# Conformer convolution on one Trainium2 core: 11 of 31 taps moved from TensorE to VectorE, ScalarE and GpSimd, and a wider second projection group

## The chip, the cores and the metric

The kernel runs on one core of one Trainium2 chip. The metric is the device time of one execution in microseconds (us). Before the change the median of three runs is 2734.93 us (2734.37 to 2735.12).

The engines are named as in the profile: PE is TensorE (PEld its weight loads), DVE is VectorE, ACT is ScalarE, POOL is GpSimd, and SP is the engine whose queue issues most transfers.

## What is computed

The reference is one step of a small hybrid decoder: an attention layer with a ConvFFN behind it, then a Conformer convolution layer with a second ConvFFN behind it. A prompt of 256 tokens and eight samples of 4 tokens share all weights, 288 columns in all. The model width is 2048, in 16 tiles of 128 channels. The change touches the Conformer layer alone:

```python
def conformer_conv(x, hist, w_pw1, b_pw1, w_dw, b_dw, ln_g, ln_b, w_pw2, b_pw2):
    a, gate = jnp.split(x @ w_pw1 + b_pw1, 2, axis=-1)
    a = a * jax.nn.sigmoid(gate)
    a_pad = jnp.concatenate([hist, a], axis=1)
    h = jax.nn.silu(layer_norm(causal_dwconv(a_pad, w_dw, b_dw), ln_g, ln_b))
    return h @ w_pw2 + b_pw2, a_pad[:, -(CONV_WIDTH - 1):]
```

`causal_dwconv` is a depthwise convolution over time with 31 taps: each output of a channel is the sum of 31 products of that channel's own values with that channel's own weights, and a bias. The history of the prompt is zero; the samples have a history of 30 rows.

## The kernel before

**Matrix products.** Channels lie on partitions and tokens along the free dimension. The core routine `gemm_gen` walks through a group of weight columns in slabs of 512 KB. For each slab, `pump` issues the transfer into a buffer `raw` (L145, SP's queue), ACT rounds it into a high part `wh` (L159), and DVE subtracts to get the low part `wl` (L161). PE then makes three matmuls per weight tile and depth step: wh by xh (L228), wh by xl (L229) and wl by xh (L230). Five `raw` and three `wh`/`wl` buffers let the split run two slabs ahead of PE, so a `wh` has to wait until PE has left the slab three before it.

**Order of the side work.** Everything else is written as generators in lanes. After each row of matmuls `tick` credits every lane with PE time and lets it issue what its credit covers (the numbers that are yielded are such times). `ev` holds the evacuation of the last group, `norms` the normalization of the layer's input, `bg` the convolutions, and `bg2` the preparation of a convolution, which starts only when `ev` is empty. All engines work in the order of issue.

**The first projection (pw1).** Group 0 holds the columns of tiles 0 and 1 and of their gates, four blocks of 128. Every later group holds one tile and its gate, two blocks. Group 0 is multiplied with the input before its normalization, and `after` (L526, L529) corrects the result. Group 1 is the first that reads the normalized input: `normed` makes it tile by tile (DVE and POOL at L484, POOL at L486, ACT at L470 and L473), ending in the low part `xl` on DVE (L476), and PE needs all 16 tiles in turn.

**The convolution of tiles 0 to 14.** `glu` makes the gated tile `apad` (sigmoid on ACT, L1552; product on DVE, L1553). `spread_out` writes it to a scratch tensor in DRAM (L1583), has POOL build small diagonal weight blocks `dg` (L1586, 1024 elements a partition), adds the samples' four products on DVE (L1573) and reads the scratch back four times with four shifts into `xt` (L1593). In `xt` 32 channels by 4 shifts fill the partitions, so that a block matmul does four taps at once; `conv` needs 8 steps of 4 column blocks, 32 matmuls (L1605). The result is evacuated by ACT for tiles 0 to 3 (L1609) and by DVE for tiles 4 to 14 (L1617 from PSUM with the centre `lnc` taken off, and L1619 for the 32 sample columns). `shifted` then feeds the layer norm's sums (ACT L298, POOL L303 and L304).

**The last tile.** `conv_last` does not go through DRAM. 14 taps (`NDG`) are full diagonal matmuls on PE (L1644), 4 (`NPOOL`) are products on ACT, added in pairs by POOL (L1640) and brought in by PE (L1646), and 13 run on DVE (L1653). Then come a sum (L1657), the last statistics matmuls (L331, L332) and the layer norm in front of pw2.

Of the kernel before, what the change touches and what calls it, by code (L numbers as in the profile page):

```python
# [7 lines left out]
F32 = mybir.dt.float32  # L8
# [4 lines left out]
AF = mybir.ActivationFunctionType  # L13
OP = mybir.AluOpType
AX = mybir.AxisListType

D = 2048
NT = 16
TP = 256
NS, TS = 8, 4  # L20
# [8 lines left out]
CW = 31  # L29
# [7 lines left out]
CH = 22  # L37
NKVB = 3
FILL = 0.45
NPOOL = 4  # L40
CAP = 3.0
SDEL = 6
TOPK = 2.6
KG = 12
DGP = 6.0
NDG = 14
CQ = 287
BIS = (1.6, 0.2)
DOTS = 0.35
ROPE = 0.8  # L50
# [8 lines left out]
CLAG = (3.2, 5.6, 5.0, 1.0)  # L59
# [474 lines left out]
def trunk(ctx, tc, a, o, stages=9):  # L534
    k = K(ctx, tc, a, o)
    nc = k.nc
# [12 lines left out]
    def halving(w, nk):  # L549
        return [k.add(Group([(w, 512 * i, 512)], [128] * 4, nk, 2)) for i in range(3)] + \  # L550
            [k.add(Group([(w, 1536 + 256 * i, 256)], [128] * 2, nk, 4)) for i in range(2)]
# [9 lines left out]
    def ffn_groups(l):  # L561
        wg, wu, wd = a["w_ffn_gate"][l], a["w_ffn_up"][l], a["w_ffn_down"][l]
        r = []
        for c in range(NF // CH):
            ga = [k.add(Group([(wg, (c * CH + 2 * i) * 128, 256), (wu, (c * CH + 2 * i) * 128, 256)],
                              [128] * 4, NT, 2)) for i in range(CH // 2)]
            wdc = wd[c * CH * 128:(c + 1) * CH * 128, :]
            gb = (halving if c and not l else narrowing)(wdc, CH)
            r.append((ga, gb))
        return r  # L570

    g_f0 = ffn_groups(0)
    g_pw1 = [k.add(Group([(a["w_pw1"], 0, 256), (a["w_pw1"], D, 256)], [128] * 4, NT, 2))]
    g_pw1 += [k.add(Group([(a["w_pw1"], 128 * j, 128), (a["w_pw1"], D + 128 * j, 128)], [128] * 2, NT, 4))
              for j in range(2, NT)]
    g_pw2 = halving(a["w_pw2"], NT)
    g_pw2[0].slabs[1].pool = True
    g_f1 = ffn_groups(1)
# [223 lines left out]
    def sample_index():  # L802
# [58 lines left out]
        def total():  # L861
            p_ = pb()
            nc.tensor.matmul(p_[:, :1], cc("bones"), cnt, start=True, stop=True)
            return p_

        nc.vector.tensor_scalar(scr, S, 0.0, 0.0, op0=OP.is_ge, op1=OP.add, accum_out=cnt)
        yield BIS[0]
        p = total()
        yield BIS[1]
        nc.vector.tensor_scalar(v, p[:, :1], float(KSEL_S), -1.0, op0=OP.is_lt, op1=OP.mult)  # L870
        for bit in range(30, -1, -1):
# [96 lines left out]
    acc = [bp.tile([128, 128 * (tt + 1)], F32, name=f"pacc{tt}") for tt in range(2)]  # L968
# [97 lines left out]
    def bank(n, bufs):  # L1066
        return pp.tile([128, 512], F32, name=n, bufs=bufs)
# [3 lines left out]
    for gi in range(2):  # L1071
# [430 lines left out]
    fp = sf.enter_context(tc.tile_pool(name="ffn0", bufs=1))  # L1502
# [15 lines left out]
    fp = sf.enter_context(tc.tile_pool(name="conf", bufs=1))  # L1518
    cy = fp.tile([128, NT, T], F32, name="cy")
    last = NT - 1  # L1520

    lpad = fp.tile([128, 286], F32, name="lpad")
    diag = fp.tile([128, NDG, 128], F32, name="diag")
    nident = fp.tile([128, 128], F32, name="nident")

    spread = tc.dram_tile([last * 128, CQ], F32, name="spread")
    zero = fp.tile([128, last, CW], F32, name="zero")
    tapm = fp.tile([128, 32], F32, name="tapm")
    wdq = fp.tile([128, NT * 32], F32, name="wdq")
    pads = {}  # L1530
# [8 lines left out]
    def glu(js, ps):  # L1539
        n = len(js)  # L1540
        for m, j in enumerate(js):
            if j == last:
                t = lpad[:, 30:]
            else:
                t = pads[j] = fp.tile([128, TP], F32, name="apad", bufs=4)
            sg = fp.tile([128, T], F32, name="sg", bufs=2)
            pa, pg_, ba, bg_ = ps[m], ps[n + m], k.par("b_pw1", j), k.par("b_pw1", 16 + j)
            if type(pa) is tuple:
                for (_, w_), b_ in ((pa, ba), (pg_, bg_)):
                    nc.gpsimd.tensor_tensor(w_, w_, b_, op=OP.add)  # L1550
                (pa, ba), (pg_, bg_) = pa, pg_
            nc.scalar.activation(sg, pg_[:, :T], AF.Sigmoid, bias=bg_)  # L1552
            nc.vector.scalar_tensor_tensor(t, pa[:, :TP], ba, sg[:, :TP], op0=OP.add, op1=OP.mult)  # L1553
            nc.vector.scalar_tensor_tensor(hist[:, j, :, CW - 1:], pa[:, TP:T].rearrange("p (s w) -> p s w", w=4),
                                           ba, sg[:, TP:].rearrange("p (s w) -> p s w", w=4),
                                           op0=OP.add, op1=OP.mult)
            yield 0.7

    def diags():
        nc.scalar.activation(nident, k.ident, AF.Copy, scale=-1.0)  # L1560
        yield DGP
        for q_ in range(NDG):
            nc.scalar.activation(diag[:, q_], k.ident, AF.Copy, scale=k.par("w_dw", last * CW + q_))
# [13 lines left out]

    def spread_out(j):

        t = pads.pop(j)  # L1580
        nc.gpsimd.tensor_copy(tailp[:, j], t[:, TP - CW + 1:])
        rows = spread[j * 128:(j + 1) * 128]
        nc.sync.dma_start(rows[:, CW:], t)  # L1583
        dg = fp.tile([128, 32, 32], F32, name="dg", bufs=2)
        wq = wdq[:, 32 * j:32 * j + 32]
        nc.gpsimd.tensor_tensor(dg, wq[:, :, None].to_broadcast([128, 32, 32]),  # L1586
                                tapm[:, None, :].to_broadcast([128, 32, 32]), op=OP.mult)
        for d in range(TS):
            samples(j, d)
            yield CLAG[0] / TS  # L1590
        xt = fp.tile([128, 4, 284], F32, name="xt", bufs=3)
        for i in range(4):
            nc.sync.dma_start(xt[32 * i:32 * i + 32], rows[:, i:i + 284].rearrange("(g c) u -> c g u", c=32))  # L1593
        yield CLAG[1]
        spreads[j] = dg, xt

    def conv(j):

        while j not in spreads:
            yield 0.3  # L1600
        dg, xt = spreads.pop(j)
        p = pp()
        for m in range(8):
            for i in range(4):
                nc.tensor.matmul(p[32 * i:32 * i + 32, :TP], dg[:, 8 * i + m], xt[:, i, 4 * m:4 * m + TP],  # L1605
                                 start=m == 0, stop=m == 7, skip_group_check=True)
        yield CLAG[2]
        if j < lnc.H:
            nc.scalar.activation(cy[:, j, :TP], p[:, :TP], AF.Identity, bias=k.par("b_dw", j))  # L1609
            yield CLAG[3]  # L1610
            lnc.first(j)
            yield 0.4
            if j == lnc.H - 1:
                for _ in lnc.center(1):
                    yield 0.4
        else:
            nc.vector.scalar_tensor_tensor(cy[:, j, :TP], p[:, :TP], k.par("b_dw", j), lnc.c[:, :TP], op0=OP.add,  # L1617
                                           op1=OP.subtract)
            nc.vector.tensor_tensor(cy[:, j, TP:], cy[:, j, TP:], lnc.c[:, TP:], op=OP.subtract)  # L1619
            yield CLAG[3]  # L1620
            lnc.shifted(j)
            yield 0.4

    def conv_last():

        j = last
        k.drain(dlane)
        npl = NPOOL
        pl = fp.tile([128, 2, TP], F32, name="pl")
        for q_ in range(NDG, NDG + npl, 2):  # L1630
            first = q_ == NDG
            d_ = pl if first else fp.tile([128, 2, TP], F32, name="tp", bufs=2)
# [9 lines left out]
        nc.tensor.matmul(pc[:, :T], nident, lnc.c, start=True, stop=False)  # L1642
        for q_ in range(NDG):
            nc.tensor.matmul(pc[:, :TP], diag[:, q_], lpad[:, q_:q_ + TP], start=False, stop=False)  # L1644
        for i in range(2):
            nc.tensor.matmul(pc[:, :TP], k.ident, pl[:, i], start=False, stop=i == 1)  # L1646
        acc = cy[:, j, :TP]
        for q_ in range(NDG + npl, CW):
            w, src = k.par("w_dw", j * CW + q_), lpad[:, q_:q_ + TP]
# [15 lines left out]
    dlane.append(diags())  # L1665
    tailp = fp.tile([128, NT, CW - 1], F32, name="tailp")
    for gi, g in enumerate(g_pw1):
        js = [0, 1] if gi == 0 else [gi + 1]
        ps = k.gemm(g, xin, pp, g is g_pw1[-1])
        k.drain(k.ev)  # L1670
        if gi == 0:
            src = []
            k.ev.append(xin.after(ps, src, fp, lambda i: cy[:, NT - 4 + i]))
            xin, ps = xin.normed(), src
        if gi == 1:
            lnc = LN(k, rp, pp, cy, CSUM, 2)
        k.ev.append(glu(js, ps))
        if js[-1] < last:
            for j in js:
                k.bg2.append(spread_out(j))  # L1680
                k.bg.append(conv(j))
# [140 lines left out]
```

## Time and profile before

| | |
|---|---|
| median of three runs | 2734.93 us |
| the profiled execution | 2738.89 us |
| its span, first to last instruction | 2737.1 us |
| PE busy in the span | 2597.2 us (95%) |
| DVE busy | 1570.6 us (57%) |
| ACT busy | 1138.6 us (42%) |
| POOL busy | 653.5 us (24%) |
| pw1 from group 1 on, with the convolutions | 1484.9 to 1742.4 us |

The span is read as a sequence of stages, each with its own limit; a busy share over the whole span says little about one of them. A row of groups gives the source line, the engine, the operation, the tiles written and read, shapes, a count, then busy time and the mean of one in ns, and behind the bar the idle time before them with what ended it. A row of waits says which engine and line waited for which, for how long in total, how often, and the longest. In a row of the timeline the start comes first, then the duration, and a square bracket holds an idle time in front. The profiled execution is 3.96 us above the median of the runs; 1.79 us of it lie outside its span.

### The profile page before, as it was taken

To read this page: it belongs to the slowest core of one execution; us is meant where nothing else is said; L and a number is where in the kernel's file an instruction comes from. 1 tells how busy PE (TensorE), PEld (TensorE's weight loads), DVE (VectorE), ACT (ScalarE), POOL (GpSimd) and SP (SyncE) were. 2 spreads that over 40 slices of the span, in tenths; PEclk is the share of its full clock that TensorE was granted. 3 is DMA by queue.
4 is the path that set the end of the run, shared out by engine and by line. 5 is a ranking of instruction groups with operands and counts; after the bars stand their busy time and mean duration, and the time that the engine had idled before them with its cause. 6 is when DMAs were issued, how large, how long until landed. Compare 5 with 4: busy or idle time off the path is not lost. (4 is left out here: it accounts for less than half of the span.)

```text
span 2737.1 us, 50293 instructions
## 1 busy us (share of the span) xinstructions
PE 2597.2 (95%) x19976; PEld 2488.5 (91%) x19976; DVE 1570.6 (57%) x2417; ACT 1138.6 (42%) x1747; POOL 653.5 (24%) x841
## 2 busy tenths in 40 slices
PE   3899798999999999999999999999999999999997
PEld 2869765899999999999998788899999999999997
DVE  2458744569666545555557455777755544555554
ACT  1344343456444334444346332555544333444433
POOL 6116524134222110111135132435111000011023
PEclk6899899999999999999999999999999999999998
DMA  5524556555555555555644666455555545555653
GB/s 166 146 78 139 185 197 244 173 168 171 183 166 171 161 163 165 168 165 165 164 161 129 163 163 166 158 170 159 171 170 163 162 158 166 168 164 163 159 176 107
DMA packets 409275, 446.94 MB, mean 163 GB/s; under 512 B 35840, under 2 KB 337584, under 8 KB 408912
## 3 DMA queue, kind: packets, MB, share of 16 engines
q1 hardware_dynamic: 396256, 397.88, 48.5%
q0 software_dynamic: 12784, 45.85, 5.4%
q8 instruction: 156, 2.56, 0.4%
q14 instruction: 79, 0.65, 0.1%
HBM read 434.54 MB, written 9.10 MB: 162 GB/s over the span
## 5 line engine op out<-in xcount | busy, mean ns | idle before, releaser
L161 DVE TENSOR_TENSOR wl<-raw,wh 128x1024 fp32r<-128x1024 f32 (+2 forms) x693 | 861.1, 1246 | 922.1 <-ACT wh L159 862.1
L159 ACT ACTIVATE wh<-raw 128x1024 fp32r<-128x1024 f32 (+1 forms) x726 | 760.7, 1051 | 1043.4 <-PE pt L229 735.2
L229 PE MATMUL pt<-xl,wh 128*128 128x288 f32 (+1 forms) x3520 | 1046.0, 297 | 8.8 <-DVE xl L476 8.7
L228 PE MATMUL pt<-xh,wh 128*128 128x288 f32 (+1 forms) x3520 | 1044.5, 297 | 0.8 <-ACT xh L1286 0.8
L230 PE MATMUL pt<-xh,wl 128*128 128x288 f32 (+1 forms) x3520 | 1042.0, 296 | 1.6 <-DVE wl L161 1.6
L229 PEld LDWEIGHTS pt<-xl,wh 128*128 128x128 f32 x3520 | 666.1, 189 | 11.5 <-DVE xl L476 11.0
L228 PEld LDWEIGHTS pt<-xh,wh 128*128 128x128 f32 x3520 | 665.5, 189 | 7.4 <-issue 6.2
L230 PEld LDWEIGHTS pt<-xh,wl 128*128 128x128 f32 x3520 | 668.4, 190 | 2.1 <-DVE wl L161 2.1
L230 PE MATMUL pt<-hh,wl 128*128 128x288 f32 (+1 forms) x1664 | 495.3, 298 | 3.6 <-DVE wl L161 3.6
L229 PE MATMUL pt<-hl,wh 128*128 128x288 f32 (+1 forms) x1664 | 495.3, 298 | 0.0
L228 PE MATMUL pt<-hh,wh 128*128 128x288 f32 (+1 forms) x1664 | 493.2, 296 | 1.2 <-ACT wh L159 1.2
L230 PEld LDWEIGHTS pt<-hh,wl 128*128 128x128 f32 x1664 | 312.8, 188 | 5.1 <-DVE wl L161 5.1
L228 PEld LDWEIGHTS pt<-hh,wh 128*128 128x128 f32 x1664 | 314.0, 189 | 2.3 <-ACT wh L159 2.1
L229 PEld LDWEIGHTS pt<-hl,wh 128*128 128x128 f32 x1664 | 313.4, 188 | 0.2
L1402 POOL COPY sto<-gpad 128x2 f32<-128x2 f32 x88 | 82.0, 932 | 964.5 <-ACT gpad L1395 964.4
L228 PE MATMUL pg<-xh,wh 128*128 128x288 f32 (+1 forms) x464 | 151.7, 327 | 26.0 <-issue 15.6
L230 PE MATMUL pg<-xh,wl 128*128 128x288 f32 (+1 forms) x464 | 143.4, 309 | 19.2 <-issue 16.7
L229 PE MATMUL pg<-xl,wh 128*128 128x288 f32 (+1 forms) x464 | 143.5, 309 | 16.4 <-issue 16.2
L228 PEld LDWEIGHTS pg<-xh,wh 128*128 128x128 f32 (+1 forms) x464 | 92.9, 200 | 35.1 <-issue 23.9
L161 POOL TENSOR_TENSOR wl<-raw,wh 128x1024 fp32r<-128x1024 f32 x33 | 80.4, 2438 | 163.6 <-DVE S L854 104.3
L1406 ACT ACTIVATE s<-y,pvec 128x304 f32<-128x304 f32 x88 | 48.4, 550 | 161.9 <-DVE y L1401 161.9
L230 PEld LDWEIGHTS pg<-xh,wl 128*128 128x128 f32 (+1 forms) x464 | 92.8, 200 | 21.8 <-issue 18.4
(378 smaller groups left out, 2397.3 us busy)
## 6 DMA issues: line engine op xcount, KB each, us to landing
raw<-w_ffn_gate SPq DMA_DIRECT2D x352, 256.0 KB
raw<-w_ffn_up SPq DMA_DIRECT2D x352, 256.0 KB
raw<-w_ffn_down SPq DMA_DIRECT2D x169, 512.0 KB
raw<-w_attn_in SPq DMA_DIRECT2D x64, 512.0 KB
raw<-w_pw SPq DMA_DIRECT2D x128, 256.0 KB
raw<-w_attn_out SPq DMA_DIRECT2D x32, 512.0 KB
raw<-w_pw SPq DMA_DIRECT2D x32, 512.0 KB
xt<-spread SPq DMA_DIRECT2D x60, 142.0 KB
```

What stands on the lines that cost most here:

```text
L159: nc.scalar.activation(wh[:, :n], r[:, :n], AF.Copy)
L161: eng.tensor_tensor(wl[:, :n], r[:, :n], wh[:, :n].bitcast(F32), op=OP.subtract)
L228: nc.tensor.matmul(out, wh[:, c:c + w], xh, start=st, stop=False)
L229: nc.tensor.matmul(out, wh[:, c:c + w], xl, start=False, stop=False)
L230: nc.tensor.matmul(out, wl[:, c:c + w], xh, start=False, stop=sp)
L1402: nc.gpsimd.tensor_copy(sto[:, j, 0:2], gp[:, 256:258])
L1406: nc.scalar.activation(s[:, :304], y[:, :304], AF.Silu, bias=k.par(bc, j))
```

## The change

Of the convolution of tiles 0 to 14, the first three of the eight matmul steps go (`PEM` = 3): 12 places, of which the first is an empty tap, so 11 taps. `dg` and `xt` shrink with it. Taps 0 to 3 become products on ACT (`NACT` = 4), the first with the bias, and three additions on POOL. Taps 4 to 10 become seven chained multiply-adds on DVE. `apad` gets 30 leading zeros, set by POOL. The convolution's PSUM result is added by DVE for all tiles; the subtraction of the centre moves to POOL ahead of the matmuls. In the last tile 10 instead of 14 taps are diagonal matmuls and 6 instead of 4 go by ACT and POOL, so DVE has 15. Group 1 of pw1 holds tiles 2 and 3, as wide as group 0, in slabs of two depth steps and 512 columns; `lnc` is made one group earlier. The yielded times of `spread_out` sum up as before, in smaller steps.

```diff
-NPOOL = 4
+NPOOL = 6
-NDG = 14
+NDG = 10
+PEM, NACT = 3, 4
...
-    g_pw1 = [k.add(Group([(a["w_pw1"], 0, 256), (a["w_pw1"], D, 256)], [128] * 4, NT, 2))]
+    g_pw1 = [k.add(Group([(a["w_pw1"], 256 * j, 256), (a["w_pw1"], D + 256 * j, 256)], [128] * 4, NT, 2))
+             for j in range(2)]
     g_pw1 += [k.add(Group([(a["w_pw1"], 128 * j, 128), (a["w_pw1"], D + 128 * j, 128)], [128] * 2, NT, 4))
-              for j in range(2, NT)]
+              for j in range(4, NT)]
...
-                t = pads[j] = fp.tile([128, TP], F32, name="apad", bufs=4)
+                pads[j] = fp.tile([128, 286], F32, name="apad", bufs=4)
+                nc.gpsimd.memset(pads[j][:, 0:30], 0.0)
+                t = pads[j][:, 30:]
...
-        dg = fp.tile([128, 32, 32], F32, name="dg", bufs=2)
-        wq = wdq[:, 32 * j:32 * j + 32]
-        nc.gpsimd.tensor_tensor(dg, wq[:, :, None].to_broadcast([128, 32, 32]),
-                                tapm[:, None, :].to_broadcast([128, 32, 32]), op=OP.mult)
+        nm = 8 - PEM
+        dg = fp.tile([128, 4, nm, 32], F32, name="dg", bufs=2)
+        wq = wdq[:, 32 * j:32 * j + 32].rearrange("p (i m) -> p i m", m=8)[:, :, PEM:]
+        nc.gpsimd.tensor_tensor(dg, wq[:, :, :, None].to_broadcast([128, 4, nm, 32]),
+                                tapm[:, None, None, :].to_broadcast([128, 4, nm, 32]), op=OP.mult)
+        tap = lambda q_: (k.par("w_dw", j * CW + q_), pad[:, q_:q_ + TP])
+        pl = fp.tile([128, TP], F32, name="ac", bufs=2)
+        for q_ in range(NACT):
+            w, src = tap(q_)
+            if q_ == 0:
+                nc.scalar.activation(pl, src, AF.Identity, bias=k.par("b_dw", j), scale=w)
+            else:
+                d_ = fp.tile([128, TP], F32, name="ad", bufs=3)
+                nc.scalar.activation(d_, src, AF.Copy, scale=w)
+                nc.gpsimd.tensor_tensor(pl, pl, d_, op=OP.add)
+            yield CLAG[0] / 8
         for d in range(TS):
             samples(j, d)
-            yield CLAG[0] / TS
+            yield CLAG[0] / 8
...
-        yield CLAG[1]
+        acc = cy[:, j, :TP]
+        for q_ in range(NACT, 4 * PEM - 1):
+            w, src = tap(q_)
+            nc.vector.scalar_tensor_tensor(acc, src, w, pl if q_ == NACT else acc, op0=OP.mult, op1=OP.add)
+            yield CLAG[1] / 7
...
+        if j >= lnc.H:
+            nc.gpsimd.tensor_tensor(cy[:, j], cy[:, j], lnc.c, op=OP.subtract)
         p = pp()
-        for m in range(8):
+        for m in range(PEM, 8):
...
+        nc.vector.tensor_tensor(cy[:, j, :TP], cy[:, j, :TP], p[:, :TP], op=OP.add)
         if j < lnc.H:
-            nc.scalar.activation(cy[:, j, :TP], p[:, :TP], AF.Identity, bias=k.par("b_dw", j))
...
-            nc.vector.scalar_tensor_tensor(cy[:, j, :TP], p[:, :TP], k.par("b_dw", j), lnc.c[:, :TP], op0=OP.add,
-                                           op1=OP.subtract)
-            nc.vector.tensor_tensor(cy[:, j, TP:], cy[:, j, TP:], lnc.c[:, TP:], op=OP.subtract)
...
-        js = [0, 1] if gi == 0 else [gi + 1]
+        js = [2 * gi, 2 * gi + 1] if gi < 2 else [gi + 2]
...
-        if gi == 1:
+        if gi == 0:
             lnc = LN(k, rp, pp, cy, CSUM, 2)
```

## Rows read from the trace of the kernel before

**Rows 1.** The page: busy time of each engine, and the chain by line.
```profile
PE 2597.2 (95%) x19976; PEld 2488.5 (91%) x19976; DVE 1570.6 (57%) x2417; ACT 1138.6 (42%) x1747; POOL 653.5 (24%) x841
PE pt L229 13%; PE pt L228 13%; PE pt L230 13%; PE pt L1605 2%; DMA raw<-w_ffn_down 1%; DVE wl L161 0%; DMA xt<-spread 0%; ACT wh L159 0%; POOL x L378 0%; PE pt L1644 0%; DMA spread<-apad 0%; SPq L1593 0%; PE pt L332 0%; DVE lnrs L348 0%; DVE xl L392 0%
```

**Rows 2.** Busy time by stage: stretch, length, engines (instructions), clock, DMA share, GB/s.
```profile
1484.90:1515.40 30.50, 20.52 (x99) 18.05 (x98) 26.92 (x38) 16.50 (x32) 20.32 (x21) 0.78 0.45 116
1515.40:1580.00 64.60, 62.91 (x649) 53.71 (x649) 28.49 (x48) 21.89 (x34) 12.25 (x13) 1.00 0.67 159
1617.94:1735.34 117.40, 116.34 (x1121) 104.88 (x1121) 63.83 (x84) 34.73 (x42) 24.16 (x27) 1.00 0.68 167
1742.40:1758.00 15.60, 11.28 (x51) 9.12 (x49) 12.62 (x28) 7.97 (x13) 4.89 (x5) 0.98 0.06 13
```

**Rows 3.** Groups by line in 1617.94:1735.34, from one convolution to the seventh after it.
```profile
L1605 PE MATMUL pt<-xt,dg 128*32 128x256 f32 x448 | 25.6, 380 | 0.9 <-DMA xt<-spread 0.7
L161 DVE TENSOR_TENSOR wl<-raw,wh 128x1024 fp32r<-128x1024 f32 x28 | 33.7, 1224 | 52.3 <-ACT wh L159 52.3
L1586 POOL TENSOR_TENSOR dg<-wdq,tapm 128x1024 f32<-128x1024 f32 x7 | 13.4, 1917 | 0.0
L1617 DVE SCALAR_TENSOR_TENSOR cy<-pt,pvec,lnc 128x256 f32<-128x256 f32 x7 | 3.3, 474 | 0.0
L303 POOL TENSOR_TENSOR lns<-lns,cy 128x288 f32<-128x288 f32 x6 | 4.9, 814 | 1.1 <-DVE cy L1619 1.1
L1573 DVE SCALAR_TENSOR_TENSOR cy<-hist,pvec,past 128x32 f32<-128x32 f32 x7 | 1.7, 240 | 0.0
```

**Rows 4.** Group 1: PE's first matmul, its largest wait, and two weight roundings that PE releases.
```profile
1484.90 0.29 PE L228 MATMUL pt<-xh,wh 128*128 128x288 f32 x1
...
PE pt L229 <- DVE xl L476: 8.7, 7, 1.9
...
1515.41 1.06 ACT L159 ACTIVATE wh<-raw 128x1024 fp32r<-128x1024 f32 x1 [7.68 <-PE pt L229]
...
1531.98 1.06 ACT L159 ACTIVATE wh<-raw 128x1024 fp32r<-128x1024 f32 x1 [2.13 <-PE pt L229]
```

**Rows 5.** Timeline of DVE and POOL: both at work on like shapes, then DVE alone.
```profile
1485.92 1.06 DVE L484 TENSOR_TENSOR x<-x,lnt 128x288 f32<-128x288 f32 x1
...
1485.65 1.02 POOL L484 TENSOR_TENSOR x<-x,lnt 128x288 f32<-128x288 f32 x1
1486.63 2.01 POOL L486 TENSOR_TENSOR x<-x,lnrs 128x288 f32<-128x288 f32 x2
...
1502.46 0.45 DVE L476 TENSOR_TENSOR xl<-x,xh 128x288 fp32r<-128x288 f32 x1
```

**Rows 6.** Timeline of one steady tile period, and L1619 once more without POOL beside it.
```profile
1642.51 1.23 DVE L161 TENSOR_TENSOR wl<-raw,wh 128x1024 fp32r<-128x1024 f32 x1 [4.09 <-ACT wh L159]
...
1644.36 1.92 POOL L1586 TENSOR_TENSOR dg<-wdq,tapm 128x1024 f32<-128x1024 f32 x1
...
1644.60 1.72 DVE L1619 TENSOR_TENSOR cy<-cy,lnc 128x32 f32<-128x32 f32 x1
...
1648.28 2.36 DVE L161 TENSOR_TENSOR wl<-raw,wh 128x1024 fp32r<-128x1024 f32 x2
...
1739.46 0.18 DVE L1619 TENSOR_TENSOR cy<-cy,lnc 128x32 f32<-128x32 f32 x1
```

**Rows 7.** The chain of the same period: start, duration, what.
```profile
1644.16 1.85 DMA spread<-apad
...
1647.41 3.71 DMA xt<-spread
...
1651.26 3.66 PE pt L1605 x64
```

**Rows 8.** Timeline of the last tile: PE, POOL and DVE.
```profile
1743.69 6.21 PE L1644 MATMUL pt<-lpad,diag 128*128 128x256 f32 x28
...
1753.03 0.65 PE L332 MATMUL pt<-lnsq,ones_d 128*128 128x288 f32 x2
...
1745.37 1.28 POOL L1640 TENSOR_TENSOR pl<-pl,tp 128x512 f32<-128x512 f32 x1 [15.02 <-ACT tp L1638]
...
1746.60 4.64 DVE L1653 SCALAR_TENSOR_TENSOR cy<-lpad,pvec,cy 128x256 f32<-128x256 f32 x9
```

More of the change, by code (lines that the diff above doesn't have):

```diff
@@ L1578, in spread_out @@
     def spread_out(j):
-        t = pads.pop(j)
+        pad = pads.pop(j)
+        t = pad[:, 30:]
         nc.gpsimd.tensor_copy(tailp[:, j], t[:, TP - CW + 1:])
@@ L1583, in spread_out @@
         nc.sync.dma_start(rows[:, CW:], t)
-        dg = fp.tile([128, 32, 32], F32, name="dg", bufs=2)
-        wq = wdq[:, 32 * j:32 * j + 32]
-        nc.gpsimd.tensor_tensor(dg, wq[:, :, None].to_broadcast([128, 32, 32]),
-                                tapm[:, None, :].to_broadcast([128, 32, 32]), op=OP.mult)
+        nm = 8 - PEM
[14 more added lines that the diff above has]
+            yield CLAG[0] / 8
         for d in range(TS):
             samples(j, d)
-            yield CLAG[0] / TS
-        xt = fp.tile([128, 4, 284], F32, name="xt", bufs=3)
+            yield CLAG[0] / 8
+        xt = fp.tile([128, 4, 284 - 4 * PEM], F32, name="xt", bufs=3)
         for i in range(4):
-            nc.sync.dma_start(xt[32 * i:32 * i + 32], rows[:, i:i + 284].rearrange("(g c) u -> c g u", c=32))
-        yield CLAG[1]
+            nc.sync.dma_start(xt[32 * i:32 * i + 32],
+                              rows[:, i + 4 * PEM:i + 284].rearrange("(g c) u -> c g u", c=32))
+        acc = cy[:, j, :TP]
[3 more added lines that the diff above has]
+            yield CLAG[1] / 7
         spreads[j] = dg, xt
@@ L1601, in conv @@
         dg, xt = spreads.pop(j)
+        if j >= lnc.H:
+            nc.gpsimd.tensor_tensor(cy[:, j], cy[:, j], lnc.c, op=OP.subtract)
         p = pp()
-        for m in range(8):
+        for m in range(PEM, 8):
             for i in range(4):
-                nc.tensor.matmul(p[32 * i:32 * i + 32, :TP], dg[:, 8 * i + m], xt[:, i, 4 * m:4 * m + TP],
-                                 start=m == 0, stop=m == 7, skip_group_check=True)
+                nc.tensor.matmul(p[32 * i:32 * i + 32, :TP], dg[:, i, m - PEM],
+                                 xt[:, i, 4 * (m - PEM):4 * (m - PEM) + TP],
+                                 start=m == PEM, stop=m == 7, skip_group_check=True)
         yield CLAG[2]
+        nc.vector.tensor_tensor(cy[:, j, :TP], cy[:, j, :TP], p[:, :TP], op=OP.add)
         if j < lnc.H:
-            nc.scalar.activation(cy[:, j, :TP], p[:, :TP], AF.Identity, bias=k.par("b_dw", j))
             yield CLAG[3]
```

## The prediction

> **What bounds the kernel now.** I read the page first. PE is busy 95% of the span, and the chain that ended last consists of its matmuls, with the convolution's line L1605 at 2% [rows 1]. So time is won where PE either does less or stops waiting. The view by stage then shows where it waits. From the start of pw1's group 1 to its end, 1484.90 to 1515.40, PE is busy 20.52 of 30.50 us at a granted clock of 0.78 (a mean of its two levels, 1.2 and 2.4 GHz), and DVE 26.92. In the steady part, 1617.94 to 1735.34, PE is busy 116.34 of 117.40 us at full clock, DVE 63.83 and POOL 24.16. After the last group there are 15.60 us with 11.28 of PE [rows 2]. These are three problems: a stage that DVE sets, a long stage that PE sets, and a tail with a chain.
>
> In the steady stretch seven tiles take 117.40 us, 16.77 each. Their seven convolutions hold 25.6 us, 3.66 each, and PE idles 0.9 us before them [rows 3]; the other 90.9 us are 28 slabs, 3.25 each or 13.0 for a group of four. Group 1 should therefore take 13.0 us and took 30.5: 17.5 us are lost. Its largest wait is PE on `xl` from DVE, 8.7 us [rows 4]; slow clock and other waits make up the rest.
>
> **Convolutions on PE.** Three of eight steps go, so 3.66 x 5/8 = 2.29 us, 1.37 less. The engine is full and nothing else ends there, so this lies on the path: 15 x 1.37 = 20.6 us, if the other engines keep up with a period of 16.77 - 1.37 = 15.40 us. Bounds: 0 (they don't) and 20.6.
>
> **What DVE and POOL get in a period.** DVE: four `wl` of 1.224 = 4.90, four sample products of 0.24 = 0.96 [rows 3], and seven taps. The last tile has the same instruction, nine in 4.64 us, 0.515 each [rows 8], so 3.61. `glu` and the PSUM addition are two reads of PSUM like L1617's 0.474 [rows 3] and a short one: 1.2. In all 10.65 us; L1619 goes. POOL: `dg` 1.917 x 5/8 = 1.20, two sums and the centre at 0.814 = 2.44 [rows 3], three additions, which I put at 0.72, between 1.28/2 = 0.64 [rows 8] and 0.814: 2.16; small copies 0.2. In all 6.0 us.
>
> What matters is whether these can run side by side. While `dg` ran, L1619, 32 columns wide, took 1.72 us; without POOL it takes 0.18 [rows 6]. L1617 in the same place, which reads PSUM, keeps 0.474 [rows 3]. So an operation of DVE with both inputs in SBUF waits for POOL. Where both are saturated, three POOL operations take 2.99 us (1485.65 to 1488.64) and DVE does one of 1.06 beside each [rows 5]: 1.0 us a pair, against 0.45 [rows 5] + 0.81 [rows 3] = 1.26 one after the other, a factor of 0.79. What contends is 10.65 - 1.2 + 6.0 = 15.45 us; times 0.79 that is 12.2, with the PSUM reads 13.4, and with 1.1 us in which DVE waits at the head of a group for `wh` (the rounding of 1.06 in [rows 4]) 14.5 us. That is under 15.40, by little.
>
> The Trainium skill speaks against the change here: "SBUF — State Buffer", section "Who interferes with whom", says that a DVE instruction with two SBUF inputs and a GpSimd instruction that reads SBUF exclude each other for whole instructions. The row of L1619 agrees, the saturated pairs only in part; by the rule taken strictly the third rival below holds.
>
> Order decides as well. DVE's next `wl` after the samples ended at about 1649.5, half of the pair at 1648.28 [rows 6]. PE needs it after the convolution, at 1651.26 + 3.66 = 1654.92 [rows 7], or 1.37 earlier now: 4.0 us of room. Ahead of it come two taps (1.0), and the first tap waits for POOL's three additions (2.16, less 0.7 that `dg` loses and less 1.5 of L1619): 1.0 to 3.2 us. That fits, barely. Behind a waiting first tap are queued the `wl` of the next slabs, for which PE's L230 waits. POOL's subtraction of the centre waits for the last tap; behind it stand only the next tile's `dg` and sums. ACT's four products, each under 0.6 us as its wider neighbours, stand in front of `wh`; ACT has a 42% share [rows 1], and I cost them at nothing; if ACT is late, `wh` costs as much. For queueing I take 2 us over all tiles (0 to 13, below).
>
> **Transfers.** The way of `apad` through DRAM starts at 1644.16, `xt` lands at 1651.12 and PE starts its convolution at 1651.26 [rows 7]: they arrive together. The same three slabs stand ahead of the convolution as before, `xt` is 272 instead of 284 columns wide, and no transfer is moved on SP. So nothing changes, but any lateness of `apad` falls on PE directly. The DMA share of 0.68 [rows 2] becomes 0.68 x 16.77/15.40 = 0.74, which leaves room.
>
> **Group 1.** With four blocks a depth step takes PE 26.0/16 = 1.6 us, not 0.8, so each `xl` is needed later. PE's work is then 26.0 + 2.3 for one convolution = 28.3 us. DVE's: the 26.92 of before [rows 2], four more `wl` (4.9), some twelve taps of tiles 0 and 1 (6.2), four more samples (1.0) and POOL's net 2 us: 41. The last 9 us of that are issued after the last `wl` of the group (two `wl`, taps, samples, POOL's share), so PE has its last `wl` at 1484.9 + 32 = 1517 and ends the slab at 1520. Before, the same eight slabs and one convolution were done when the rounding at 1531.98 was released [rows 4]. 1531.98 - 1520 = 12.0, of which 1.4 is the convolution counted above: 10.6 us won. Bounds: PE alone, 1513.2, gives 17.4; DVE to the end of its 41 us, 1526, gives 4.6. I take 10.6, in the middle, because DVE's sum is of rows but its order is a guess.
>
> **Backlog.** Two tiles instead of one follow at once, each group's lane works off 1.25 tiles for some five groups, and the centring of the first four tiles falls among them. Contended work is near PE's there. I take 3 us lost (0 to 6).
>
> **The last tile.** Four diagonal taps of 6.21/14 = 0.44 leave PE, but DVE gets two more of 0.515, and a second POOL addition of 1.28 holds DVE up by about 1.0. Before, DVE ended at 1751.24 and PE with L332 at 1753.68 [rows 8], nearly a tie; now DVE ends at 1753.3 and alone sets the end. I take 1.7 us lost (0 to 2.0; PE's shorter queue gives some back).
>
> **Sum.** 20.6 + 10.6 - 2 - 3 - 1.7 = 24.5 us. Of the profiled execution's 2738.89 that leaves 2714.4; the median is 3.96 lower, so 2734.93 - 24.5 = **2710.4 us**.
>
> **Rivals.** (1) **Group 1 wins nothing**: DVE, with 41 us, stays the bound and the backlog eats the rest. For it: DVE was busy 26.92 of 30.50 us. Against it: twice the matmuls per `xl`. 24.5 - 10.6 = 13.9: 2721.0 us. (2) **All bounds good**: 20.6 + 17.4 = 38: 2697 us. For it: DVE in the steady stretch is idle 46%. (3) **DVE and POOL exclude each other**: the place is L161 behind the taps, the price the plain sum 10.65 + 6.0 + 1.1 = 17.75 us a period, and it decides as soon as this exceeds 16.77. Tiles 4 to 14 then lose 11 x 0.98 = 10.8; with group 1 at 4.6, the backlog at 6 and 1.7 at the end (tiles 0 to 3 at nothing), 13.9 us slower: 2748.8 us. For it: L1619's 1.72. Against it: the factor of 0.79. (4) **No visible gain**: the PSUM reads alone overlap, 17.75 - 1.2 = 16.55, so 11 x 0.2 = 2.2 won, 4.6 in group 1, 6 and 1.7 lost: 2736 us. That the change doesn't do what it says I leave out: the matmuls do go from the loop.
>
> **Chances.** Forecast 0.45 (its own range 2704 to 2716), rival 1 0.20, rival 2 0.10, rival 4 0.11, rival 3 0.14. 0.2%, or 5.5 us, is about what a measurement of this kernel can tell from no change. Forecast and rivals 1 and 2 are faster by more: 0.75; rival 4 is the same, 0.11; rival 3 slower, 0.14. The range reaches from rival 2's end, 2696, to 2733; outside lie rival 3 and half of rival 4, 0.2.
>
> **What would show it.** Right: L1605 with 600 instructions and about 34 us; convolutions 15.4 us apart in the steady stretch with PE over 97% busy; group 1 ending near 1520; L161 not over about 1.35 us. Wrong: PE's L230 waiting for `wl`, or L1605 for `xt`, by tens of us in all (rivals 3, 4); group 1 with PE waiting for `xl` as before (rival 1). If DVE's taps took well over 0.6 us each beside POOL, the sum per period would be wrong, and with it the forecast.

## The result and the profile after

The changed kernel takes 2707.94 us in the median of four runs (2706.6 to 2710.55), the kernel before 2734.65 beside it: a ratio of 0.9906 with a 95% interval of 0.9889 to 0.9923, or 26.7 us less. In a later set of runs the same pair gave 0.9924 (0.9909 to 0.994), 21.5 us by the medians. The forecast was 24.5 us less, 2710.4 us. The profiled execution of after has a span of 2706.3 us.

The lines of `kernel.py` have moved: the convolution's matmul is L1629 (before L1605), the taps on DVE L1615, the additions on POOL L1603, POOL's subtraction of the centre L1625, the weight split L160 and L162, the three matmuls L229 to L231.

Busy time of each engine on the page of after, which answers to [rows 1]:

```profile
PE 2567.1 (95%) x19608; PEld 2467.9 (91%) x19608; DVE 1631.4 (60%) x2517; ACT 1160.7 (43%) x1801; POOL 697.8 (26%) x913
```

Busy time by stage, as in [rows 2]: group 1 with the first convolution in it, from its first matmul to its last, and the steady stretch from convolution 8 to 14:

```profile
1477.56:1516.50 38.94, 30.85 (x234) 28.58 (x232) 36.13 (x58) 24.45 (x46) 25.03 (x31) 0.96 0.52 142
1613.13:1705.80 92.67, 91.87 (x816) 84.61 (x817) 77.71 (x111) 39.92 (x60) 40.91 (x52) 1.00 0.71 183
```

In the steady stretch six tiles take 92.67 us, 15.45 each; before, the same six (1634.53 to 1735.34) took 100.81, 16.80 each. PE is as full as before and DVE has gone from 54% busy [rows 2] to 84% (77.71 of 92.67). Group 1 now holds 8 slabs and a convolution, 26.0 + 2.4 us of PE at full clock, and takes 38.9; before, this work took 47.0 (to the rounding at 1531.98 [rows 4]). PE waits 8.0 us in it:

```profile
PE pt L231 <- DVE wl L162: 4.3, 4, 2.2
PE pt L1629 <- DMA xt<-spread: 3.7, 1, 3.7
```

Groups by line in the steady stretch of after, as in [rows 3]:

```profile
L162 DVE TENSOR_TENSOR wl<-raw,wh 128x1024 fp32r<-128x1024 f32 x24 | 29.2, 1219 | 13.4 <-ACT wh L160 13.4
L1615 DVE SCALAR_TENSOR_TENSOR cy<-apad,pvec,cy 128x256 f32<-128x256 f32 x39 | 20.9, 536 | 0.9
L1629 PE MATMUL pt<-xt,dg 128*32 128x256 f32 x240 | 14.2, 381 | 0.7 <-DMA xt<-spread 0.7
L1603 POOL TENSOR_TENSOR ac<-ac,ad 128x256 f32<-128x256 f32 x18 | 13.3, 737 | 0.9
L1625 POOL TENSOR_TENSOR cy<-cy,lnc 128x288 f32<-128x288 f32 x6 | 10.3, 1723 | 29.9 <-DVE cy L1615 29.9
L1592 POOL TENSOR_TENSOR dg<-wdq,tapm 128x640 f32<-128x640 f32 x6 | 7.7, 1276 | 0.0
L1577 DVE SCALAR_TENSOR_TENSOR cy<-hist,pvec,past 128x32 f32<-128x32 f32 x6 | 6.9, 1144 | 0.0
```

A convolution holds PE 14.2/6 = 2.37 us (3.66 before), a tap costs DVE 0.536, an addition POOL 0.737, and `dg` fell from 1.917 to 1.276. L162 still idles before it for ACT: DVE is waiting there, and not late. A sample product of 32 columns takes 1.144 us instead of 0.240: it starts beside POOL's `dg` and ends when `dg` ends (one runs from 1668.57 to 1669.72, beside a `dg` from 1668.40 to 1669.68). The first of the seven taps, which has a row of its own (it reads `ac`), takes 0.928.

The last tile of after, on DVE, POOL and PE, as in [rows 8]:

```profile
1715.77 6.57 DVE L1675 SCALAR_TENSOR_TENSOR cy<-lpad,pvec,cy 128x256 f32<-128x256 f32 x11
...
1714.53 2.84 POOL L1662 TENSOR_TENSOR pl<-pl,tp 128x512 f32<-128x512 f32 x2 [5.41 <-ACT tp L1660]
...
1722.95 0.97 PE L332 MATMUL pt<-cy,ones_d 128*128 128x288 f32 x2 [2.46 <-DVE cy L1679]
```

PE has done its part and waits 2.46 us for DVE's sum: the near tie of before is decided.

**One measure for all runs.** The code ahead of group 1 and behind the first matmul of pw2 is not changed, yet these parts differ from execution to execution: group 1 begins at 1484.90 in the profile before and 1477.56 after. I therefore take, from each trace, the stretch from group 1's first matmul to pw2's first matmul, and in it the starts of convolutions 0, 8 and 14, all counted from group 1's first matmul. "8 slabs" is the end of the 192nd weight matmul: the wide group 1, or the two narrow groups with the same number of matmuls, with convolution 0 among them in every run:

| run | convolution 0 | 8 slabs | convolution 8 | 14 | pw2 | from 14 to pw2 |
|---|---|---|---|---|---|---|
| before | 35.3 | 47.2 | 149.6 | 250.4 | 273.1 | 22.7 |
| before_again | 35.4 | 47.2 | 149.6 | 249.5 | 272.1 | 22.7 |
| after | 26.0 | 39.1 | 135.5 | 228.2 | 251.7 | 23.4 |
| after_again | 26.3 | 39.9 | 136.0 | 228.3 | 251.4 | 23.1 |
| wide_only | 26.6 | 41.7 | 144.1 | 244.6 | 267.3 | 22.7 |
| taps_only | 35.3 | 45.9 | 144.7 | 237.3 | 260.4 | 23.1 |
| old_tail | 26.2 | 40.1 | 137.2 | 229.4 | 250.8 | 21.4 |
| old_tail_again | 26.0 | 39.1 | 135.2 | 226.9 | 248.3 | 21.4 |
| pem4 | 26.5 | 40.6 | 145.0 | 239.5 | 263.2 | 23.7 |
| dve_all | 26.2 | 40.0 | 136.9 | 229.3 | 252.3 | 23.1 |
| no_adds | 26.0 | 39.8 | 136.1 | 229.2 | 252.3 | 23.1 |
| late_conv0 | 34.2 | 42.4 | 138.2 | 230.2 | 251.6 | 21.4 |
| late_glu0 | 28.1 | 34.9 | 131.1 | 223.5 | 244.8 | 21.4 |

Repeats of one kernel agree within 2.5 us at pw2. By this measure the change wins 273.1 - 251.7, or 21.5 us before rounding.

### The profile page after: what moved, and what is told of

Its sections match the earlier page's. It is cut to its first block, busy times and chain, and to the rows that moved or that the text cites. A ratio compares the mean times of both kernels' runs of the same rounds, so it can differ in the third digit from the quotient of the medians.

```text
span 2706.3 us, 49786 instructions
## 1 busy us (share of the span) xinstructions
PE 2567.1 (95%) x19608; PEld 2467.9 (91%) x19608; DVE 1631.4 (60%) x2517; ACT 1160.7 (43%) x1801; POOL 697.8 (26%) x913
## 4 chain that ended last, share of the span: by engine, by line
PE 78%; DVE 3%; POOL 2%; DMA 1%; issue 1%; ACT 1%; SPq 0%; another core or an unknown queue 0%; ACTq 0%; DVEq 0%; POOLq 0%
PE pt L231 24%; PE pt L230 24%; PE pt L229 24%; DVE wl L162 1%; PE tr L1169 1%; PE pt L1629 1%; PE m L1233 1%; PE sc L1190 1%; POOL x L487 0%; ACT wh L160 0%; PE q L1141 0%; DMA xt<-spread 0%; PE tr L1119 0%; DMA kvx<-kvc,idxS 0%; DVE cy L1675 0%
## 5 line engine op out<-in xcount | busy, mean ns | idle before, releaser
L162 DVE TENSOR_TENSOR wl<-raw,wh 128x1024 fp32r<-128x1024 f32 (+2 forms) x693 | 864.6, 1250 | 832.0 <-ACT wh L160 797.5
L160 ACT ACTIVATE wh<-raw 128x1024 fp32r<-128x1024 f32 (+1 forms) x726 | 760.2, 1051 | 994.6 <-PE pt L230 690.7
L231 PE MATMUL pt<-xh,wl 128*128 128x288 f32 (+1 forms) x3520 | 1040.5, 296 | 5.5 <-DVE wl L162 5.4
L229 PE MATMUL pt<-xh,wh 128*128 128x288 f32 (+1 forms) x3520 | 1042.3, 296 | 0.8 <-ACT xh L1288 0.8
L231 PEld LDWEIGHTS pt<-xh,wl 128*128 128x128 f32 x3520 | 666.2, 189 | 7.3 <-DVE wl L162 7.3
L229 PEld LDWEIGHTS pt<-xh,wh 128*128 128x128 f32 x3520 | 663.4, 188 | 7.4 <-issue 6.2
L231 PE MATMUL pt<-hh,wl 128*128 128x288 f32 (+1 forms) x1664 | 495.4, 298 | 2.9 <-DVE wl L162 2.9
L229 PE MATMUL pt<-hh,wh 128*128 128x288 f32 (+1 forms) x1664 | 493.2, 296 | 1.2 <-ACT wh L160 1.2
L231 PEld LDWEIGHTS pt<-hh,wl 128*128 128x128 f32 x1664 | 312.8, 188 | 3.9 <-DVE wl L162 3.9
L229 PEld LDWEIGHTS pt<-hh,wh 128*128 128x128 f32 x1664 | 313.5, 188 | 2.3 <-ACT wh L160 2.1
L229 PE MATMUL pg<-xh,wh 128*128 128x288 f32 (+1 forms) x464 | 152.3, 328 | 25.2 <-issue 15.0
L231 PE MATMUL pg<-xh,wl 128*128 128x288 f32 (+1 forms) x464 | 144.0, 310 | 18.5 <-issue 16.0
L230 PE MATMUL pg<-xl,wh 128*128 128x288 f32 (+1 forms) x464 | 144.1, 311 | 16.4 <-issue 16.3
L229 PEld LDWEIGHTS pg<-xh,wh 128*128 128x128 f32 (+1 forms) x464 | 93.4, 201 | 33.6 <-issue 22.6
L162 POOL TENSOR_TENSOR wl<-raw,wh 128x1024 fp32r<-128x1024 f32 x33 | 80.9, 2452 | 162.4 <-DVE S L856 102.6
L231 PEld LDWEIGHTS pg<-xh,wl 128*128 128x128 f32 (+1 forms) x464 | 93.3, 201 | 21.0 <-issue 16.4
## 6 DMA issues: line engine op xcount, KB each, us to landing
xt<-spread SPq DMA_DIRECT2D x60, 136.0 KB
```

The source lines that it names most:

```text
L160: nc.scalar.activation(wh[:, :n], r[:, :n], AF.Copy)
L162: eng.tensor_tensor(wl[:, :n], r[:, :n], wh[:, :n].bitcast(F32), op=OP.subtract)
L229: nc.tensor.matmul(out, wh[:, c:c + w], xh, start=st, stop=False)
L230: nc.tensor.matmul(out, wh[:, c:c + w], xl, start=False, stop=False)
L231: nc.tensor.matmul(out, wl[:, c:c + w], xh, start=False, stop=sp)
```

## The experiments

**Where group 1 starts when nothing is changed.** No edit; the kernel before.

> The kernel before once more, unchanged: where its group 1 starts. In the two profiles it starts at 1484.90 before and at 1477.56 after, though nothing ahead of it is changed. Theory A (executions differ by some us in the stage before, and the profiled one of before was a late one): a start between 1478 and 1484, the stretch behind it 273 us again. Rival B (something ahead of it was changed by the edit): 1485 again.

On that chip everything ahead was some 70 us shorter (group 1 at 1409.08), so the start can't be compared with 1485. The stretch behind it came out at 272.1 us. The other runs of that chip tell the rivals apart better: with edits behind them they begin group 1 at 1408.52 (taps_only), 1410.47 (wide_only) and 1415.52 (old_tail), and the unedited kernel lies among them, which speaks against rival B. On the chip of the last three runs the starts lie at 1480.17 to 1482.38, on that of the four before them at 1475.98 to 1481.47, all with the same code ahead. A start may lie 7 us off for no reason of the kernel's, nearly as much as in the pair of profiles with which I started.

Where it goes can be read from the starts of the weight roundings. The 11th starts at 91.9 to 93.4 us in the profiles at 1476 to 1485, and at 40.5 to 41.2 in the four of the short chip: 51 of the 70 us. In the nine profiles of the first kind the 61st starts at 329.1 to 331.8 and the 81st at 532.7 to 542.1; from there to group 1 it is 941 to 944 in all of them. So in those nine profiles the scatter arises in the stage between 330 and 540 us, ahead of everything that was edited. What causes either is open.

**The wide group alone.**

```diff
 # the kernel before
-    g_pw1 = [... tiles 0 and 1] + [one tile each, j in range(2, NT)]
+    g_pw1 = [... two tiles each, j in range(2)] + [one tile each, j in range(4, NT)]
-        js = [0, 1] if gi == 0 else [gi + 1]
+        js = [2 * gi, 2 * gi + 1] if gi < 2 else [gi + 2]
...
-        if gi == 1:
+        if gi == 0:
             lnc = LN(k, rp, pp, cy, CSUM, 2)
```

> The kernel before with pw1's group 1 as wide as group 0 (and lnc made one group earlier), no tap moved. Measure: the stretch from group 1's first matmul to pw2's first matmul, 273.1 us before and 251.7 after the whole change. Theory A (the wide group spreads the need for xl over twice the matmuls and wins by itself): 8 slabs and one convolution take some 34 us instead of 47.0, the stretch is 260 to 264 us, the median some 10 us under before. Rival B (the width only serves the taps, by itself it is neutral): the stretch stays within 3 us of 273.

267.3 us, and a ratio of 0.9978 (0.9966 to 0.999): it wins by itself, 5.3 us by the stretch and 4.6 by the medians, half of what theory A wanted. The 8 slabs are done 5.5 us earlier, convolution 8 starts 5.5 us earlier, and nothing changes behind. PE's own two waits in its group 1:

```profile
PE pt L230 <- DVE wl L161: 5.1, 4, 2.2
PE pt L1606 <- DMA xt<-spread: 4.3, 1, 4.3
```

The wait for `xl` [rows 4] is gone; `wl` and `xt` have taken its place, and PE idles as long as before. By stage, over the 8 slabs and one convolution, before_again and then wide_only, on the same chip:

```profile
1409.08:1456.30 47.22, 37.70 (x260) 33.48 (x259) 33.29 (x49) 22.15 (x41) 22.41 (x23) 0.82 0.56 139
1410.47:1452.10 41.63, 32.25 (x258) 28.95 (x256) 31.63 (x46) 21.48 (x40) 20.86 (x21) 0.96 0.51 136
```

PE is idle 9.5 us in the first and 9.4 in the second. What shrank is its busy time for the same matmuls, 37.70 to 32.25 us, with the granted clock at 0.82 and at 0.96. So the 5.5 us were won through the clock, and not, as theory A had it, through shorter waits. In the narrow groups PE had stopped eight times, seven of them for `xl`; in the wide one it stopped five times.

**The taps alone.**

```diff
 # the changed kernel
-    g_pw1 = [... two tiles each, j in range(2)] + [one tile each, j in range(4, NT)]
+    g_pw1 = [... tiles 0 and 1] + [one tile each, j in range(2, NT)]
-        js = [2 * gi, 2 * gi + 1] if gi < 2 else [gi + 2]
+        js = [0, 1] if gi == 0 else [gi + 1]
```

> The whole change but with the narrow groups of before (tiles 2 and 3 in groups of their own). Theory A (the parts add up: group 1 loses its 17.5 us as before): the stretch from group 1's first to pw2's first matmul is 251.7 + 10 to 14 = 262 to 266 us, the median 2717 to 2722. Rival B (the gain is that of the taps, the width does nothing): 252 to 254 us, median 2708 to 2711. Rival C (DVE can't hold the taps beside the normalization without the wide group): over 270 us.

260.4 us and 0.9955 (0.9938 to 0.9971): 12.2 us under the 272.6 of both runs of before, a little better than theory A's 262 to 266. The parts add up to 5.3 + 12.2 = 17.5, and together they win 21.1 of the same 272.6 (251.5 in the mean of two runs). The 3.6 us between them lie little above the 2.5 by which repeats differ, so that the parts help each other is likely, not shown. Its group 1 is that of before; by stage, with the columns of [rows 2]:

```profile
1408.52:1439.00 30.48, 20.83 (x100) 18.64 (x99) 28.38 (x42) 18.43 (x37) 22.18 (x27) 0.72 0.44 117
```

and by its largest wait, as in [rows 4]:

```profile
PE pt L230 <- DVE xl L477: 8.4, 6, 3.8
```

**The last tile as before.**

```diff
 # the changed kernel
-NPOOL = 6
+NPOOL = 4
-NDG = 10
+NDG = 14
-            d_ = pl if first else fp.tile([128, 2, TP], F32, name="tp", bufs=2)
+            d_ = pl if first else fp.tile([128, 2, TP], F32, name="tp", bufs=1)
```

> The whole change, but the last tile is done as before: 14 diagonal taps on PE, 4 by ACT and POOL, 13 on DVE (one buffer less for a tile that is used once). From the last convolution's start to pw2's first matmul it is 22.70 us before (with 1.37 more convolution) and 23.44 after. Theory A (DVE sets the end of the last tile, two more taps and one more POOL addition cost 2.1): 21.3 us, and the median 2 us lower, 2706. Rival B (the last tile is bound elsewhere): 23 to 23.5 us and no difference.

> The whole change with the last tile done as before, once more and with more rounds. If the 2.05 us that the stretch behind the last convolution showed are real: the median 1 to 3 us under that of the whole change on the same chip, the stretch behind the last convolution 21.3 to 21.4 us again.

Both times 21.4 us behind the start of the last convolution, against 23.4 and 23.1: theory A, 1.9 us on the average. In the timeline of PE (old_tail) no wait stands in front of the last pair:

```profile
1658.04 1.02 PE L1668 MATMUL pt<-pl,ident 128*128 128x256 f32 x4
...
1661.33 0.65 PE L333 MATMUL pt<-lnsq,ones_d 128*128 128x288 f32 x2
```

The medians on one chip are 2709.41 us with the old last tile and 2711.27 for the whole change; 1.9 us lie inside what the runs scatter (0.9904 to 0.9934 against 0.9909 to 0.994). The traces show it; the times alone don't.

**The whole change again.** No edit.

> The whole change once more, beside the variants on one chip: stretch from group 1 to pw2 251.6 us again (within 1 us), 21 to 25 us under before in the median.

251.4 us, ratio 0.9924: as expected.

**One step more off PE.**

```diff
 # the changed kernel
-PEM, NACT = 3, 4
+PEM, NACT = 4, 4
-            yield CLAG[1] / 7
+            yield CLAG[1] / 11
```

> The whole change with four of eight steps off PE: 15 taps moved, 4 to ACT and POOL, 11 to DVE. The steady period from convolution 8 to 14 is 15.45 us after the change and 16.8 before; PE alone would need 13.07 + 3.66/2 = 14.9. Theory A (DVE and POOL overlap at the factor 0.79; DVE is busy 77.7 us of six periods, 12.95 each, and idle 2.5): four more taps of 0.536 make 15.1, right at PE's 14.9: a period of 15.0 to 15.5, little or nothing won over the whole change, and the stretch from group 1 to pw2 as long or some us longer (251 to 258) since the first tiles come doubled. Rival B (exclusion for whole instructions: the plain sum 10.65 + 6.0 + 2.1): a period over 17. Rival C (DVE has room enough): 14.9.

Its steady stretch by stage, and the convolution's group in it:

```profile
1623.88:1718.38 94.50, 89.57 (x768) 83.73 (x769) 92.06 (x136) 39.27 (x60) 39.66 (x52) 1.00 0.72 180
```

```profile
L1629 PE MATMUL pt<-xt,dg 128*32 128x256 f32 x192 | 11.6, 381 | 4.4 <-DMA xt<-spread 4.4
```

15.75 us a period, above theory A's 15.0 to 15.5 and far from rival B's 17: DVE is now busy 92.06 of 94.50 us and sets the pace, and PE stands before each convolution since `apad`, and so `xt`, come late. The stretch is 263.2, 5 us over what I had allowed: most of it is lost ahead of convolution 8 (145.0 instead of 135.5), where the first tiles come doubled and PE's largest wait is 6.3 us for one of DVE's sums (L279). So in this order of the side work the change's three steps are the last that fit.

**All eleven taps on DVE.**

```diff
 # the changed kernel
-PEM, NACT = 3, 4
+PEM, NACT = 3, 0
...
-            nc.vector.scalar_tensor_tensor(acc, src, w, pl if q_ == NACT else acc, op0=OP.mult, op1=OP.add)
+            if q_ == 0:
+                nc.vector.tensor_scalar(acc, src, w, k.par("b_dw", j), op0=OP.mult, op1=OP.add)
+            else:
+                nc.vector.scalar_tensor_tensor(acc, src, w, acc, op0=OP.mult, op1=OP.add)
...
```

> The whole change, but all 11 moved taps run on DVE (the first with the bias), none on ACT and POOL. Theory A (in the steady stretch PE is the bound, and what DVE gains of its own work, four taps, 2.1 us, it gets back from POOL's three additions that no longer hold it up): period 15.4 as after the change, DVE busy 12.3 to 13.5 a period, the stretch from group 1 to pw2 250 to 254 us. Rival B (DVE's own instructions bound the stage and the share of ACT and POOL is needed): a period over 16, the stretch over 258.

Its steady stretch by stage:

```profile
1618.37:1710.77 92.40, 91.84 (x820) 84.86 (x823) 79.16 (x135) 29.78 (x36) 26.95 (x34) 1.00 0.72 184
```

Theory A: 15.40 a period, 252.3 in all, and DVE at 79.16/6 = 13.2 us a period against 12.95 with four taps fewer of its own. Four taps more cost DVE 0.24 us a period and not 2.1: the rest it had paid before in waiting for POOL's additions. The share of ACT and POOL in the taps wins nothing that these runs show (251.7 and 251.4 us with it).

**POOL's additions left out.**

```diff
 # the changed kernel
                 nc.scalar.activation(d_, src, AF.Copy, scale=w)
-                nc.gpsimd.tensor_tensor(pl, pl, d_, op=OP.add)
```

> The whole change without POOL's three additions per tile (taps 1 to 3 are computed by ACT and left out of the sum). It takes away what DVE's first tap waits for and most of what shares the SBUF reads with it. Theory A (they cost DVE time but end nothing that counts in the steady stretch): DVE's samples (L1577) fall from 652 to 1144 ns a piece to under 500, DVE busy from 12.95 to about 11 us a period, the period stays 15.4, and the stretch from group 1 to pw2 falls by at most 3 us from 251.6. Rival B (DVE and POOL set the period): the period falls under 15.2.

Its steady stretch by stage, and two groups in it:

```profile
1614.39:1707.49 93.10, 91.82 (x816) 84.89 (x816) 69.02 (x110) 39.93 (x60) 21.71 (x34) 1.00 0.71 182
```

```profile
L1624 POOL TENSOR_TENSOR cy<-cy,lnc 128x288 f32<-128x288 f32 x6 | 4.8, 802 | 35.5 <-DVE cy L1614 35.5
L1577 DVE SCALAR_TENSOR_TENSOR cy<-hist,pvec,past 128x32 f32<-128x32 f32 x6 | 6.9, 1145 | 0.0
```

The period stays at 15.52 and the stretch at 252.3: the additions end nothing that counts. DVE's busy time falls by 8.7 us where POOL's additions were 13.3, so DVE paid 0.65 us for each microsecond of them. In one point I was wrong: the first sample product did not get short (1.145 us as before). It is `dg` that holds it, and not the additions. POOL's subtraction of the centre fell from 1.723 to 0.802, now that it no longer meets a `wl`.

**The first convolution later.**

```diff
 # with the last tile as before
         dg, xt = spreads.pop(j)
+        if j == 0:
+            yield 4.0
```

> The whole change with the last tile done as before (14 diagonal taps, 4 by ACT and POOL), and tile 0's convolution issued 4 units, some 4.4 us of matmuls, later. After the change PE stands 3.7 us in front of this convolution for xt, in the middle of group 1. Theory A (its place in PE's order is too early, since apad is late by DVE's backlog): the wait goes, the stretch from group 1 to pw2 is 249.6 - 3.5 = 246 us (250.8 in the run with the old last tile alone). Rival B (PE only meets the next late wl instead): 249 to 251.

Theory A fell: 251.6 us, a little over rival B's range too. The wait for `xt` is gone, the 8 slabs are done at 42.4 instead of 39.1 and 40.1, and PE's waits of group 1 are

```profile
PE pt L231 <- DVE wl L162: 8.0, 5, 2.9
PE pt L229 <- ACT wh L160: 2.2, 1, 2.2
```

PE only met the next late thing. The rounding `wh` among them pointed at ACT. In the changed kernel's group 1 the timeline of ACT shows this:

```profile
1489.69 1.04 ACT L160 ACTIVATE wh<-raw 128x1024 fp32r<-128x1024 f32 x1
1494.76 1.28 ACT L1556 ACT_TABLE_LOAD   x1 [4.02 <-DVE cy L530]
...
1500.90 1.99 ACT L160 ACTIVATE wh<-raw 128x1024 fp32r<-128x1024 f32 x2
```

For 10 us no weight is rounded. ACT waits for DVE's correction of group 0 (L530) in front of the gate of tiles 0 and 1, and two roundings stand behind it. SP's queue stands in front of the first write of `apad` in the same way (its longest wait there), though in this run no rounding of the group is seen waiting for a transfer:

```profile
SPq L1588 <- DVE apad L1557: 13.9, 1, 13.9
```

**The first gate later.**

```diff
 # with the last tile as before
         n = len(js)
+        if js[0] == 0:
+            yield 5.0
         for m, j in enumerate(js):
```

> The whole change with the last tile done as before, and the gate of tiles 0 and 1 issued 5 units, some 5.5 us of matmuls, later. After the change ACT stands 4.0 us in front of this sigmoid for DVE's correction of group 0, then loads a table, and two roundings of weights behind it come at 1500.9 while PE waits for their wl; SP's weight transfers stand behind the first write of apad in the same way. Theory A (PE's loss in group 1 is this order: weights behind the gate): the roundings go ahead, PE's waits in group 1 shrink by 3 to 5 us, the stretch from group 1 to pw2 is 246 to 248 us (250.8 and 251.6 in the runs with the old last tile). Rival B (DVE's amount of work in the stage is the bound, whatever the order): 250 to 253, as with the later convolution.

244.8 us, better than theory A's 246 to 248. On ACT one more rounding now comes before the gate, and the next one right behind its first half:

```profile
1497.91 1.05 ACT L160 ACTIVATE wh<-raw 128x1024 fp32r<-128x1024 f32 x1
1499.56 1.28 ACT L1558 ACT_TABLE_LOAD   x1 [0.60 <-DVE cy L530]
...
1501.29 1.04 ACT L160 ACTIVATE wh<-raw 128x1024 fp32r<-128x1024 f32 x1
```

PE's waits in its group 1:

```profile
PE pt L231 <- DVE wl L162: 3.7, 3, 2.2
PE pt L1631 <- DMA xt<-spread: 0.3, 1, 0.3
```

PE's waits in group 1 fall from 8.0 to 4.0 us, and the 8 slabs with the first convolution are done after 34.9 us instead of 39.1. By stage:

```profile
1482.38:1517.31 34.93, 30.93 (x236) 28.89 (x235) 34.68 (x48) 24.65 (x47) 24.73 (x31) 0.95 0.49 141
```

PE is as long busy as in after, old_tail and their repeats (30.8 to 31.0 us, at 0.96), so here it is the waits that shrank. One thing clouds the cause. The taps of tiles 0 and 1 hang on their gate: in the same stretch DVE now does 7 taps and 4 sample products, where it did 12 and 8 (old_tail_again, 36.98 us busy), and the rest comes behind the group. So weights went ahead of other work on ACT, on SP and on DVE at once; which of the three queues was worth how much is not shown. DVE is busy 34.68 of 34.93 us and now leaves no room.

The stretch is 4.8 us under the 249.6 of the two runs with the old last tile, 3.5 under the one on the same chip. This is the fastest version: 2703.04 us, ratio 0.9889 (0.9872 to 0.9907), against 0.9919 with the old last tile alone and 0.9924 of the change on the same chip.

## Why the prediction held, point by point

| step | forecast | measured in the stretch |
|---|---|---|
| convolutions, 15 tiles | 20.6 | 19.4 (15 x 1.29) |
| queueing in the steady stretch | -2 | +0.4 |
| group 1 | +10.6 (4.6 to 17.4) | +6.7 |
| backlog of the first tiles | -3 (0 to 6) | -3.0 |
| last tile | -1.7 (0 to 2.0) | -2.0 |
| sum | 24.5 | 21.5 |

The measured column is before against after: a convolution went from 3.66 to 2.37 us; the other rows are what is left of the four stretches of the table above (to the 8 slabs, to convolution 8, to 14, to pw2) when 1.29 for each convolution in them is taken off.

**Convolutions.** The period fell from 16.80 to 15.45 us in the first pair of profiles and from 16.64 to 15.39 in their repeats, 1.25 to 1.35 a tile, against 1.37 forecast. The engines kept up: this step was right in its mechanism, and a little large, since five of eight steps take 2.37 us and not 2.29. The work put on DVE was forecast at 13.4 us a period with POOL's share in it, and DVE was busy 12.95; the tap was 0.536 for 0.515, the addition 0.737 for 0.72, `dg` 1.276 for 1.20. That sum is better than its parts: the four sample products were put at 0.24 each from a row that shows one of the four [rows 3], and took 3.35 us a tile in all after the change. The wait for `wl` that I feared did not come; I had taken 2 us for it.

**DVE beside POOL.** A 32-column product takes 1.144 us next to `dg` and 0.240 without it [rows 3]. The Trainium skill, "SBUF — State Buffer", section "Who interferes with whom", calls the port pair that DVE and GpSimd share an exclusive lock, and says that a DVE instruction with two SBUF inputs contends with a GpSimd instruction that reads SBUF. The trace agrees for this single instruction, which waits for the whole of `dg`. Taken as a plain sum, exclusion would have made the period 17.75 us, and it was 15.45: DVE paid 0.65 us for each microsecond of POOL's additions (no_adds), and had the time. My third rival therefore fell. The factor of 0.79 from the saturated pairs came out near enough in the total; by itself it was not measured again. With one step more DVE is 97% busy and the period rises to 15.75 (pem4): the point at which DVE sets the period lies between three steps and four.

**Group 1.** This term was mis-sized: 6.7 us for 10.6. I gave PE the end of group 1 after 35 us; it came after 39. Two things are in the 4 us. PE was busy 30.85 us (the first row by stage above) and not 28.3, at a clock of 0.96 for which I had priced nothing in this stage; and it waited 8.0 us for `wl` and `xt`, where my sum left it 6.8. The mechanism was not quite mine either: the wide group wins its 5.5 us by PE's busy time at a higher clock, and not by shorter waits (wide_only). The waits hang on the order of issue, which I had called a guess: with the first gate later the group ends after 34.9 us, about the forecast (late_glu0). How much of that is ACT's queue, SP's or DVE's is open. The prediction had listed who stands behind a waiting first tap, but not who stands behind the gate, which was in front of the weights before as well. My second thought, that moving the convolution alone would take PE's wait away, was wrong (late_conv0).

**Backlog and last tile.** Between the 8 slabs and convolution 8 the change wins 6.0 us where seven convolutions are worth 9.0, so 3.0 are lost, as forecast. In the last tile DVE sets the end, as forecast.

**The sum.** By the stretch the change wins 21.5 us, 3.0 under the forecast; by the first medians 26.7, 2.2 over it, and by the repeat 21.5. The agreement of the first medians is in part luck: some 5 us of it lie in parts that the change doesn't touch, and in the stretch itself group 1, 3.9 us short, and the queueing that did not come, 2.4 us better, go against each other.

**The other rivals.** Group 1 winning nothing (2721) fell with the 6.7 us that it won, though DVE was busy 36.13 of its 38.94 us, so its amount of work stood close behind. No visible gain (2736) wanted a period of 16.55 and had 15.45. All bounds good (2697) wanted PE alone as the bound of group 1; waits of 8.0 us stood against it.

## What to carry to other kernels

Before work is moved off the engine that bounds a stage, add up what the receiving engine does in one period, with its waiting for POOL in it, and compare it with the new, shorter period: here 13.4 against 15.4 held, and one step more did not. Then look at what stands in each in-order queue behind an instruction that waits; issuing an early gate, and with it all that hangs on it, some 5 us later won 4.8 of 249.6 us with no work saved. Look at the clock of a stage beside its waits: the wide group won by the one and not by the other. Where the untouched parts of a kernel scatter by more than the effect, measure between two fixed instructions of the trace.

## What the runs showed of the hardware

Parts of the kernel that no edit touched took up to 7 us more or less from one execution to the next on one chip (group 1 starting at 1408.52 to 1415.52 in four runs), and some 70 us less on this chip than on others; 51 of the 70 lie in the first 93 us. The same matmuls of pw1's first 8 slabs kept PE busy 37.70 us at a granted clock of 0.82 and 32.25 at 0.96. DVE's additional busy time from POOL's additions was 8.7 us for 13.3 us of them, and POOL is held up in turn: the same 288-column subtraction took it 1.723 us when it met a `wl` and 0.802 when it did not.
